# Which engine computes the first norm's adaLN columns: six columns from GpSimd to TensorE, and where the bias is added

## The chip, the cores and the metric

The kernel runs on one NeuronCore of a Trainium2 chip. The metric is device time in microseconds (us). Before the change it is 1839.2 us, the median of 3 runs (1838.87 to 1846.52). Engines are named as in the profile: PE is TensorE's matmuls and PEld its weight loads, DVE is VectorE, ACT ScalarE, POOL GpSimd, SP SyncE, which here only issues DMAs.

## The reference, cut to what matters

Two layers of a transformer over 128 context tokens and 512 latent tokens, 1024 features. Each layer first turns the two conditioning vectors (one for each stream) into shift, scale and gate, and each of its two norms is modulated by them:

```
mod = silu(cond) @ w_ada[l] + b_ada[l]           # 6 * 1024 values for each of two conds
sa, ca, ga, sf, cf, gf = split(mod, 6)
h = rmsnorm(x) * g_mix[l] * (1 + ca) + sa
p = h @ w_in[l]                                  # then attention, Fourier mixing, w_out, FFN
```

`sa` and `ca` of layer 0 (2 x 1024 values for each conditioning vector) are wanted before the first projection can begin.

## The kernel before, in words

Features lie on the 128 partitions, so a vector of 1024 values is eight columns, and the 6144 values of `mod` are 48 columns `mods[:, l, j]`, each with two entries (one a stream). Columns 0 to 7 are `sa`, 8 to 15 `ca`. A column needs a 128x1024 weight tile (512 KB) and can be computed in three ways.

- `ada_dve` (L146): two multiply-and-sum instructions on VectorE (L149; the trace calls them CUSTOM_DVE_ANT_0), then a 128x2 add of the bias on VectorE (L152).
- `ada_pool` (L156): two 128x1024 multiplications on GpSimd (L159), a sum over each product on ScalarE (L160), the bias on VectorE (L161).
- `ada_pe` (L165): eight fp32 matmuls with the weight tile as stationary operand and two moving columns (L168), into one PSUM tile; the bias on VectorE (L169). The trace shows such a matmul as two records, so a column is x16 there and x8 in the program's order.

At the start, `first()` loads x, sums its squares and computes the reciprocal roots (`stats`, L221). Then `norm_first` (L432) goes over the eight feature tiles k. For each, `before(k)` (L778) computes columns k and 8+k by the two letters of `ADA_ENG[k]` and folds the scale with the norm's gain (`make_gain`, L171). `modulate` (L242) writes the tile as two parts hi and lo (`hh_n`, `hl_n`), and 12 matmuls (`mm3`, L131 to L133) add this tile's part of the first two projections into the PSUM tiles `pk` and `pq`: two halves of the tokens, two projections, three products each. That is 96 matmuls of 320 or 322 columns, and `pk` and `pq` are complete only after the last. I call this the norm stage.

The weight tiles of the 16 columns take slots that attention uses later, seven at a time, in the order of `slots` (L775). SP issues the loads in its program order, and a load waits for its slot's last reader. The PSUM tiles of `ada_pe` alternate between two slots of one buffer each (tags `av` and `mm`).

The Tile framework's scheduler puts the instructions of the whole program in an order for each engine, and each engine then runs its list strictly in order. A change in one place can so reorder the lists elsewhere.

Two later places use the same helpers. In attention of layer 0, `gate` computes columns 16 to 23 with `ada_pe`. In `ffn(0)` the columns 24 to 39 are computed while the output projection (`wo`) runs, by `ADA2_ENG` alternately on VectorE and GpSimd; I call it the wo stage. It has two halves of tokens, with a `stats` between them (`ms` L229, `rs` L232, `rb` L234) whose result `rb` TensorE's matmul L237 waits for. The other columns, up to the whole of layer 1, are computed by `ada_dve` under the FFN.

Of the kernel before, what the change touches and what calls it, by code (L numbers as in the profile page):

```python
# [25 lines left out]
NL_TOK = 512  # L26
# token columns of a feature-major tile: ctx 0:128, two spare columns, latent 130:642
TW = 642
LO = 130
# the same with two zero columns at either end, for the convolution  # L30
HW = 646
# [6 lines left out]
FGROUPS = ((0, 8), (8, 8), (16, 6))  # L38
# head-key columns: latent 0:512, cache 512:640, ctx 640:768
KW = 768  # L40
# [5 lines left out]
def backbone_kernel(ctx: ExitStack, tc: tile.TileContext, A, O):  # L46
# [9 lines left out]

# [1 line left out]
    def const(name, shape):  # L58
# [20 lines left out]
    def late_consts(tmp):  # L79
        lam = tmp("lamv")[:, :L * 128].rearrange("p (l a d) -> p l a d", l=L, a=4)  # L80
        nc.sync.dma_start(out=lam, in_=A["lam"])
        for nm, sh in (("cos", [P, NL_TOK]), ("sin", [P, NL_TOK]), ("perm", [P, P]),
                       ("sel", [P, 2]), ("scv", [P, 1]), ("g_sub", [P, L]), ("g_kv", [P, L]),
                       ("g_ffn", [P, L, NK]), ("g_fin", [P, NK])):
            C[nm] = const(nm, sh)
        # lambda and the gain of the sub-norm, per layer
        lamt = tmp("lamt")[:, :L * 64].rearrange("p (l a d) -> p l a d", l=L, a=2)
        nc.vector.tensor_tensor(out=lamt, in0=lam[:, :, 0::2, :], in1=lam[:, :, 1::2, :], op=ALU.mult)
        lams = gp.tile([P, L, 2], F32, name="lams")
        nc.vector.tensor_reduce(out=lams, in_=lamt, axis=AX.X, op=ALU.add)  # L90
        nc.scalar.activation(out=lams, in_=lams, func=AF.Exp)
        neglam = gp.tile([P, L], F32, name="neglam")
        nc.vector.tensor_tensor(out=neglam, in0=lams[:, :, 1], in1=lams[:, :, 0], op=ALU.subtract)
        gs = gp.tile([P, L], F32, name="gs")
        for l in range(L):
            li = 0.8 - 0.6 * math.exp(-0.3 * l)
            nc.vector.tensor_scalar(out=neglam[:, l:l + 1], in0=neglam[:, l:l + 1], scalar1=-li, scalar2=None,
                                    op0=ALU.add)
            nc.vector.tensor_scalar(out=gs[:, l:l + 1], in0=C["g_sub"][:, l:l + 1], scalar1=1.0 - li, scalar2=None,
                                    op0=ALU.mult)  # L100
        C["neglam"], C["gs"] = neglam, gs

# [1 line left out]
    @contextmanager  # L104
# [9 lines left out]

    # the slots of weight tiles: two of each kind throughout, more in a phase that has the room
    def raw_tile(pool=None, bufs=2):
# [22 lines left out]

    # adaLN columns as per-partition scalars, on VectorE (features over partitions)  # L140
    def ada_cond(t):
# [4 lines left out]
    def ada_dve(l, j, wt, scond, junk):  # L146
        nc.sync.dma_start(out=wt, in_=A["w_adaT"][l, j])
        for c in range(2):
            nc.vector.tensor_tensor_reduce(  # L149
                out=junk, in0=wt, in1=scond[:, c], op0=ALU.mult, op1=ALU.add,  # L150
                scale=1.0, scalar=0.0, accum_out=mods[:, l, j, c:c + 1])
        nc.vector.tensor_scalar(out=mods[:, l, j], in0=mods[:, l, j], scalar1=bada[:, l, j:j + 1], scalar2=None,  # L152
                                op0=ALU.add)

    # the same on GpSimd and ScalarE
    def ada_pool(l, j, wt, scond, prod):  # L156
# [6 lines left out]

    # the same on TensorE, for some of the first layer's columns
    def ada_pe(j, wt, t):  # L165
        nc.sync.dma_start(out=wt, in_=A["w_ada0"][j])
        for k in range(NK):
            nc.tensor.matmul(t, lhsT=wt[:, 128 * k:128 * k + 128], rhs=scT[:, k], start=k == 0, stop=k == NK - 1)  # L168
        nc.vector.tensor_scalar(out=mods[:, 0, j], in0=t, scalar1=bada[:, 0, j:j + 1], scalar2=None, op0=ALU.add)  # L169

# [8 lines left out]

    # reciprocal root mean square of the columns of sq (features over partitions), one per  # L180
    # token, spread over the partitions: returns psum access patterns (ctx, latent)
    def rstd_bcast(sq, rhs, n, width, pool, eps=None, lat=None):
        """rhs [P, n]: which features a column sums."""
        pc, pl = tpt("rsc"), (lat or tpt)("rsl")
# [21 lines left out]

    # squares of the columns o:o+w of feature tile m: the first seven are summed in acc, the
    # last stays by itself
    def sumsq(acc, xm, m, pool, o, w, eng=None):
# [8 lines left out]

    # the statistics of half the columns (those before or from column bd): the reciprocal root
    # mean squares over the partitions, as (column, width, stream, psum access pattern)  # L220
    def stats(hf, bd, sqs, pool):  # L221
# [20 lines left out]

    # norm and modulation of half of feature tile k, into the tiles hi and lo
    def modulate(l, n, k, x, rb, hh, hl, pool, lo_pool=False):
# [18 lines left out]

# [1 line left out]
    def attention(l, xs, rb, close_x):  # L265
        with tc.tile_pool(name=f"at{l}", bufs=1, side="left", reuse_waits="tile") as ap, \
# [4 lines left out]
            mq = dp.tile([6, P, 2, TW], F32, name=f"mq_{l}")  # L271
            # rows 64 to 96 of a key hold the turned latent ones, rows 96 to 128 the others: nought elsewhere
            mk = dp.tile([6, P, 2, KW], F32, name=f"mk_{l}")
# [36 lines left out]

            # one 128-feature tile of the input projection, features over partitions
            def proj(j, wide=False, mid=None, dst=None, scale=None):
# [26 lines left out]

            # x32 columns: rotated latent 0:512, [cache], ctx, spare, raw latent  # L340
            def rotate(x32, lat0, j, pe=False):
# [88 lines left out]

            # the norm, with the first two projections on its heels
            def norm_first(before):  # L432
# [39 lines left out]

            # softmax numerators of one block of scores; their sums go to s_out
            def soft(s_in, p_out, s_out):
# [4 lines left out]

            # MLA: the normalised map. Differential: sum1 * (map1 - lambda * map2); sum1 stays in  # L480
            # the sums of the head and is allowed for in the epsilon of its norm.
            def combine(Ps, ss, w, qt):
# [18 lines left out]

            # scores(i, qt, tile) fills a psum tile with map i of query tile qt (4: ctx)
            def attend(nmap, scores, vv, p, e, of, sums=None):
# [115 lines left out]

            # keys and values of a pair of heads, in four steps  # L620
            def mla_kv(p):
# [55 lines left out]

            # Fourier mixing. The latent columns are folded by the symmetry of the transform over
            # positions: sums and differences of columns t and 512 - t, and of rows of the result.
            def fourier_u(mid):  # L680
# [14 lines left out]
            def fourier(u, oh, ol):  # L695
# [32 lines left out]
                for g in range(2):  # L728
# [10 lines left out]
                    w = slice(128 * g, 128 * g + 128)  # L739
                    # position 256 has no odd part: it goes where that of position 0, nought, lies  # L740
                    e = slice(1280, 1282)
# [20 lines left out]
            if l == 0:  # L762
# [10 lines left out]
                junk = ap.tile([P, 2 * 642], BF16, name="junk0", tag="t640", bufs=T640_BUFS)[:, :D]  # L773
                prod = ap.tile([P, 2, BW], F32, name="prod", tag="base", bufs=2)[:, :, :D]
                slots = iter((("VV", 6 * 256, NPAIR), ("ks", 2 * KW, 2), ("x32", BW, 2), ("VV", 6 * 256, NPAIR),  # L775
                              ("ks", 2 * KW, 2), ("x32", BW, 2), ("VV", 6 * 256, NPAIR)) * 3)

                def before(k):  # L778
                    for j, eng in zip((k, 8 + k), ADA_ENG[k]):
                        tag, n, b = next(slots)  # L780
                        t = ap.tile([P, n], F32, name="ada0", tag=tag, bufs=b)[:, :D]
                        if eng == "P":
                            ada_pe(j, t, (avt if j % 2 else mmt)("adaps")[:, :2])
                        elif eng == "V":
                            ada_dve(0, j, t, scond, junk)
                        else:
                            ada_pool(0, j, t, scond, prod)
                    make_gain(0, 0, k, k + 1)
# [65 lines left out]

# [1 line left out]
    xspill = dp.tile([NK, P, TW], F32, name="xspill")  # L856
# [12 lines left out]
    def first():  # L869
        xs, accs, close = x_pool("xin")  # L870
        # scratch: the slots of the tiles that the norm fills last
        class Pl:
# [182 lines left out]
PE_ROT = 1  # L1055
ADA_ENG = ('VG', 'GP', 'GV', 'GP', 'VV', 'PP', 'GV', 'PG')
T640_BUFS = 6
# [6 lines left out]

# [1 line left out]
def _split12(x):  # L1066
# [6 lines left out]
def _tables():  # L1073
# [3 lines left out]
    ang = {0: (t // 64).astype(f)[None, :] * inv[:, None], 1: (t % 64).astype(f)[None, :] * inv[:, None]}  # L1077
    # rows: half of a rotated pair, axis, frequency, then four blocks of 32 features
    blk = np.repeat(np.concatenate([ang[0], ang[1]] * 2, 0), 4, 0)
# [35 lines left out]

# the order of the rotated features: row (h, x, d, block) holds feature (block, x, h, d)
_ROT = np.arange(P).reshape(4, 2, 2, 8).transpose(2, 1, 3, 0).reshape(P)
# [78 lines left out]
```

## Time and profile before

| what | value |
|---|---|
| median of 3 runs | 1839.2 us |
| profiled execution, first to last instruction | 1843.6 us |
| PE busy | 1717.2 us (93%) |
| DVE busy | 1166.4 us (63%) |
| ACT busy | 779.4 us (42%) |
| POOL busy | 650.0 us (35%) |
| norm stage (end of the statistics' matmuls to the last of `pq`) | 19.6 to 74.2 us |
| wo stage on a saturated DVE | 394 to 460 us |

The page's span is the only time that the profiled execution has; it lies 4.4 us above the median of the runs. Starts in the rows are us from the span's start. A timeline row gives start, busy time, engine, line, operation, output and inputs, shapes and, in brackets, the idle time before it and what ended it. Busy times of pipelined matmuls overlap, so the pace of TensorE is read from one start to the next.

### The profile page before, as it was taken

What the parts mean: (1) busy time and instruction counts of PE and PEld (TensorE: products, weight loads), DVE (VectorE), ACT (ScalarE), POOL (GpSimd) and SP (SyncE); (2) the same over time, 40 slices, a digit from 0 to 9 for tenths busy, and PEclk for the clock granted to TensorE, in tenths of its full rate; (3) what the DMA queues carried; (4) which work ended last, traced back from release to release, by engine and by line L of the source; (5) the groups of instructions that cost most, each with busy time, mean ns of one, the idle gap of its engine ahead of it and who ended that gap; (6) DMA issues with size and microseconds to landing.
All of it is one profiled execution on the core that took longest, in us unless ns stands there. A gap on an engine that the chain in (4) does not pass through costs nothing. (4 is left out here: it accounts for less than half of the span.)

```text
span 1843.6 us, 29032 instructions
## 1 busy us (share of the span) xinstructions
PE 1717.2 (93%) x11160; PEld 1670.1 (91%) x11160; DVE 1166.4 (63%) x2051; ACT 779.4 (42%) x1494; POOL 650.0 (35%) x719
## 2 busy tenths in 40 slices
PE   6988899986999999999999798999999999999997
PEld 5878899876899999999998787998999999999997
DVE  7628765679799999734455388865544434443445
ACT  5436564643543123313343466765433313321332
POOL 6547454548422112201242576562212201220222
PEclk9889898988899999999999899999999999999998
DMA  7367654655255565322254576562312222222223
GB/s 279 96 210 208 193 172 149 207 175 171 82 182 172 183 202 164 111 73 73 63 169 135 177 214 183 176 205 73 103 35 74 76 72 78 70 81 69 78 69 118
DMA packets 81084, 249.70 MB, mean 135 GB/s; under 512 B 10417, under 2 KB 19761, under 8 KB 79281
## 3 DMA queue, kind: packets, MB, share of 16 engines
q1 hardware_dynamic: 74226, 209.13, 35.6%
q0 software_dynamic: 6720, 38.72, 7.6%
q8 instruction: 88, 1.44, 0.3%
q14 instruction: 50, 0.41, 0.1%
HBM read 203.43 MB, written 41.24 MB: 133 GB/s over the span
## 5 line engine op out<-in xcount | busy, mean ns | idle before, releaser
L132 PE MATMUL up<-hl_o,whi 128*128 128x324 f32 x1408 | 441.2, 314 | 2.7 <-POOL hl_o L113 2.7
L131 PE MATMUL up<-hh_o,whi 128*128 128x324 f32 x1408 | 440.4, 314 | 2.3 <-ACT hh_o L260 1.2
L133 PE MATMUL up<-hh_o,wlo 128*128 128x324 f32 x1408 | 440.8, 314 | 0.0
L112 ACT CAST whi<-raw 128x1024 fp32r<-128x1024 f32 (+2 forms) x210 | 207.0, 989 | 434.7 <-PE dn L132 204.7
L113 DVE TENSOR_TENSOR wlo<-raw,whi 128x1024 fp32r<-128x1024 f32 (+2 forms) x184 | 227.0, 1237 | 203.4 <-ACT whi L112 199.2
L990 POOL TENSOR_TENSOR cg<-cg,cv 128x644 f32<-128x644 f32 x44 | 73.2, 1664 | 665.4 <-DVE cv L986 653.9
L132 PEld LDWEIGHTS up<-hl_o,whi 128*128 128x128 f32 x1408 | 268.0, 190 | 4.4 <-POOL hl_o L113 4.3
L131 PEld LDWEIGHTS up<-hh_o,whi 128*128 128x128 f32 x1408 | 267.8, 191 | 3.0 <-ACT hh_o L112 1.6
L133 PEld LDWEIGHTS up<-hh_o,wlo 128*128 128x128 f32 x1408 | 267.1, 190 | 0.0
L131 PE MATMUL dn<-gh,whi 128*128 128x322 f32 x704 | 218.7, 314 | 5.0 <-ACT gh L112 3.9
L132 PE MATMUL dn<-gl,whi 128*128 128x322 f32 x704 | 220.1, 313 | 0.0
L133 PE MATMUL dn<-gh,wlo 128*128 128x322 f32 x704 | 218.9, 313 | 0.0
L149 DVE CUSTOM_DVE_ANT_0 junk<-ada,scond 128x1024 bf16<-128x1024 f32 x138 | 199.4, 1445 | 4.4 <-ACT scond L143 2.8
L477 DVE TENSOR_REDUCE nm<-sc 128x1 f32<-128x640 f32 (+1 forms) x180 | 126.5, 711 | 76.5 <-PE sc L576 56.2
L478 ACT ACTIVATE P<-sc,nm 128x640 f32<-128x640 f32 (+1 forms) x180 | 128.1, 713 | 74.9 <-DVE nm L477 56.6
L859 DVE SCALAR_TENSOR_TENSOR x_x<-dn,mods,x_x 128x128 f32<-128x128 f32 (+2 forms) x144 | 57.6, 436 | 132.8 <-PE dn L133 132.7
L131 PEld LDWEIGHTS dn<-gh,whi 128*128 128x128 f32 x704 | 133.4, 190 | 6.9 <-ACT gh L112 4.1
L133 PEld LDWEIGHTS dn<-gh,wlo 128*128 128x128 f32 x704 | 133.8, 190 | 0.4 <-DVE wlo L113 0.4
L132 PEld LDWEIGHTS dn<-gl,whi 128*128 128x128 f32 x704 | 133.9, 190 | 0.3 <-POOL gl L113 0.2
L131 PE MATMUL proj<-hh_n,whi 128*128 128x320 f32 (+1 forms) x320 | 109.0, 341 | 5.7 <-ACT whi L112 3.0
L133 PE MATMUL proj<-hh_n,wlo 128*128 128x320 f32 (+1 forms) x320 | 106.8, 334 | 0.0
L132 PE MATMUL proj<-hl_n,whi 128*128 128x320 f32 (+1 forms) x320 | 106.5, 333 | 0.0
(299 smaller groups left out, 3740.0 us busy)
## 6 DMA issues: line engine op xcount, KB each, us to landing
raw<-in_w_up SPq DMA_DIRECT2D x88, 512.0 KB, 3.6
ada<-in_w_adaT SPq DMA_DIRECT2D x83, 512.0 KB, 3.6
raw<-in_w_down SPq DMA_DIRECT2D x32, 512.0 KB, 3.6
raw<-in_w_in SPq DMA_DIRECT2D x28, 512.0 KB, 4.9
raw<-in_w_down SPq DMA_DIRECT2D x32, 384.0 KB, 3.2
qs<-dq POOLq DMA_DIRECT2D x12, 865.5 KB, 9.1
ks<-mk POOLq DMA_DIRECT2D x12, 768.0 KB, 4.9
raw<-in_w_out SPq DMA_DIRECT2D x16, 512.0 KB, 4.5
```

The source lines that it names most:

```text
L112: nc.scalar.copy(out=hi, in_=src)
L113: (lo_eng or nc.vector).tensor_tensor(out=lo, in0=src, in1=hi.bitcast(F32), op=ALU.subtract)
L131: nc.tensor.matmul(out, lhsT=lh, rhs=rh, start=first, stop=False)
L132: nc.tensor.matmul(out, lhsT=lh, rhs=rl, start=False, stop=False)
L133: nc.tensor.matmul(out, lhsT=ll, rhs=rh, start=False, stop=last)
L149: nc.vector.tensor_tensor_reduce(out=junk, in0=wt, in1=scond[:, c], op0=ALU.mult, op1=ALU.add, scale=1.0, scalar=0.0, accum_out=mods[:, l, ...
L477: nc.vector.tensor_reduce(out=nm, in_=s_in, axis=ax, op=ALU.max, negate=True)
L478: nc.scalar.activation(out=p_out, in_=s_in, func=AF.Exp, bias=nm, scale=1.0, accum_out=s_out)
L859: nc.vector.scalar_tensor_tensor(out=x[:, o:o + w], in0=ps, scalar=gate, in1=x[:, o:o + w], op0=ALU.mult, op1=ALU.add)
L990: nc.gpsimd.tensor_tensor(out=c[0], in0=c[0], in1=c[1], op=ALU.mult)
```

## The change

`ADA_ENG` gives eleven of the sixteen columns to TensorE, five to VectorE (as before) and none to GpSimd; before it was five, five and six. `ada_dve` passes the bias as the initial value of its sums in place of 0.0, so L152 goes everywhere (5 in the norm stage, 8 in the wo stage, 56 more). `ada_pe` adds the bias on ScalarE, as an Identity activation that reads PSUM (new L167), also for the eight columns of `gate`. `ada_pool` stays in the wo stage as it was. Comments go, so line numbers move by two to five.

```diff
@@ ada_dve
             nc.vector.tensor_tensor_reduce(
                 out=junk, in0=wt, in1=scond[:, c], op0=ALU.mult, op1=ALU.add,
-                scale=1.0, scalar=0.0, accum_out=mods[:, l, j, c:c + 1])
-        nc.vector.tensor_scalar(out=mods[:, l, j], in0=mods[:, l, j], scalar1=bada[:, l, j:j + 1], scalar2=None,
-                                op0=ALU.add)
+                scale=1.0, scalar=bada[:, l, j:j + 1], accum_out=mods[:, l, j, c:c + 1])
@@ ada_pe
-        nc.vector.tensor_scalar(out=mods[:, 0, j], in0=t, scalar1=bada[:, 0, j:j + 1], scalar2=None, op0=ALU.add)
+        nc.scalar.activation(out=mods[:, 0, j], in_=t, func=AF.Identity, bias=bada[:, 0, j:j + 1], scale=1.0)
@@ attention, before(k)
-                prod = ap.tile([P, 2, BW], F32, name="prod", tag="base", bufs=2)[:, :, :D]
...
                         if eng == "P":
                             ada_pe(j, t, (avt if j % 2 else mmt)("adaps")[:, :2])
-                        elif eng == "V":
+                        else:
                             ada_dve(0, j, t, scond, junk)
-                        else:
-                            ada_pool(0, j, t, scond, prod)
@@
-ADA_ENG = ('VG', 'GP', 'GV', 'GP', 'VV', 'PP', 'GV', 'PG')
+ADA_ENG = ('VP', 'PP', 'PV', 'PP', 'VP', 'PV', 'PP', 'PV')
```

The first place is PE at the start of the norm stage, from the last statistics to the first projection matmuls (`rsh` and `rb` are the statistics, `adaps` the columns' PSUM tile, `ada` their weight tile). Before:

```order
L226 MATMUL rsh<-ones,sq_123 128x1
L168 MATMUL adaps<-c_condT,ada_264 128x2 x8
L237 MATMUL rsh<-ident,rb_136 128x128 x2
L237 MATMUL rsh<-ident,rb_136 128x63
L237 MATMUL rsh<-ident,rb_152 128x128 x2
L237 MATMUL rsh<-ident,rb_152 128x65
L131 MATMUL pk<-hh_n_171,whi 128x320
L131 MATMUL pq<-hh_n_171,whi 128x320
```

The same place now, up to the same two matmuls:

```order
L224 MATMUL rsh<-ones,sq_123 128x1
L166 MATMUL adaps<-c_condT,ada_205 128x2 x7
L235 MATMUL rsh<-ident,rb_136 128x128 x2
L235 MATMUL rsh<-ident,rb_136 128x63
L166 MATMUL adaps<-c_condT,ada_205 128x2
L166 MATMUL adaps<-c_condT,ada_260 128x2 x3
L235 MATMUL rsh<-ident,rb_152 128x128 x2
L235 MATMUL rsh<-ident,rb_152 128x65
L166 MATMUL adaps<-c_condT,ada_260 128x2 x5
L166 MATMUL adaps<-c_condT,ada_318 128x2 x8
L131 MATMUL pk<-hh_n_171,whi 128x320
L131 MATMUL pq<-hh_n_171,whi 128x320
```

Where one column stood ahead of the first projection matmul, three stand now. The second place is PE between the first and the second feature tile (`hh_n_171` and `hh_n_172`), as one piece of the difference:

```order
 L132 MATMUL pq<-hl_n_179,whi 128x322
 L133 MATMUL pq<-hh_n_171,wlo 128x322
+L166 MATMUL adaps<-c_condT,ada_272 128x2 x6
+L166 MATMUL adaps<-c_condT,ada_425 128x2 x8
+L166 MATMUL adaps<-c_condT,ada_366 128x2 x8
+L166 MATMUL adaps<-c_condT,ada_517 128x2 x8
 L131 MATMUL pk<-hh_n_172,whi 128x320
 L131 MATMUL pq<-hh_n_172,whi 128x320
-L168 MATMUL adaps<-c_condT,ada_447 128x2 x4
```

Nearly four columns come here in one stretch, with no projection matmul among them. The third place is DVE between the two halves of the wo stage, from the statistics `ms` to `rb` (`x2_x0`, `x3_x0` are residual tiles). Before:

```order
L229 TENSOR_SCALAR ms_4686<-rsh_4679 128x3
L152 TENSOR_SCALAR mods_81<-mods_81,c_b_ada_66 128x2
L149 ISA junk_4302,mods_81<-ada_4667,scond_4299 128x1024
L149 ISA mods_81 128x1
L859 SCALAR_TENSOR_TENSOR x2_x0_4279<-wo_4857,mods_81,x2_x0_4279 128x320
```

The same place now, with the new kernel's line numbers:

```order
L227 TENSOR_SCALAR ms_4702<-rsh_4695 128x3
L149 ISA junk_4326,mods_81<-ada_4684,scond_4323,c_b_ada_66 128x1024
L149 ISA mods_81 128x1
L854 SCALAR_TENSOR_TENSOR x2_x0_4303<-wo_4873,mods_81,x2_x0_4303 128x320
L149 ISA junk_4326,mods_81<-ada_4684,scond_4323,c_b_ada_66 128x1024
```

The 128x2 bias add is gone from DVE's list and the multiply-and-sum reads `c_b_ada` itself.

## Rows read from the trace of the kernel before

**Rows 1.** Busy time by stretch: length, PE, PEld, DVE, ACT, POOL, granted clock, DMA

```profile
19.60:35.60 16.00, 6.24 (x28) 6.05 (x28) 15.85 (x23) 4.40 (x10) 14.51 (x16) 1.00 0.90 334
35.60:74.20 38.60, 35.57 (x160) 34.26 (x160) 35.30 (x80) 21.17 (x48) 20.63 (x13) 0.82 0.18 60
394.00:460.00 66.00, 43.22 (x262) 41.77 (x261) 65.77 (x72) 26.50 (x46) 58.67 (x40) 0.83 0.53 177
```

**Rows 2.** Timeline of PE in the norm stage

```profile
19.00 0.57 PE L226 MATMUL rsh<-ones,sq 128*128 128x1 f32 x2
20.28 3.57 PE L168 MATMUL adaps<-c_condT,ada 128*128 128x2 f32 x16 [0.71 <-DMA ada<-in_w_ada]
23.71 2.80 PE L237 MATMUL rsh<-ident,rb 128*128 128x128 f32 x12
35.62 0.64 PE L131 MATMUL pk<-hh_n,whi 128*128 128x320 f32 x1 [9.10 <-ACT hh_n L260]
...
40.80 0.47 PE L131 MATMUL pk<-hh_n,whi 128*128 128x322 f32 x1
41.07 0.47 PE L131 MATMUL pq<-hh_n,whi 128*128 128x322 f32 x1
...
51.71 0.36 PE L132 MATMUL pq<-hl_n,whi 128*128 128x322 f32 x1
51.91 0.31 PE L133 MATMUL pq<-hh_n,wlo 128*128 128x322 f32 x1
54.35 1.96 PE L168 MATMUL adaps<-c_condT,ada 128*128 128x2 f32 x12 [2.13 <-DVE mods L169]
...
60.16 0.64 PE L132 MATMUL pk<-hl_n,whi 128*128 128x322 f32 x1 [0.65 <-DVE hl_n L261]
...
62.37 3.58 PE L168 MATMUL adaps<-c_condT,ada 128*128 128x2 f32 x16 [0.24 <-DVE mods L169]
65.80 0.61 PE L132 MATMUL pk<-hl_n,whi 128*128 128x320 f32 x1
...
69.04 0.31 PE L132 MATMUL pk<-hl_n,whi 128*128 128x320 f32 x1
69.19 0.31 PE L133 MATMUL pk<-hh_n,wlo 128*128 128x320 f32 x1
...
73.92 0.30 PE L133 MATMUL pq<-hh_n,wlo 128*128 128x322 f32 x1
```

**Rows 3.** Costliest groups of DVE, 14 to 74 us

```profile
L149 DVE CUSTOM_DVE_ANT_0 junk<-ada,scond 128x1024 bf16<-128x1024 f32 x10 | 20.8, 2081 | 0.1
```

**Rows 4.** Line L149 in the whole run: ns min/median/max

```profile
L149 DVE CUSTOM_DVE_ANT_0 junk<-ada,scond x138: 1204/1214/3414, 14.1 to 752.4; 128x1024 bf16<-128x1024 f32 x138
```

**Rows 5.** Line L166, the loads of TensorE's columns: landing

```profile
DMA to landing us min/median/max: 3.4/4.4/9.7
```

**Rows 6.** Timeline of ACT: a small activation, and the end of the norm stage

```profile
36.88 0.20 ACT L91 ACTIVATE lams<-lams 128x4 f32<-128x4 f32 x1
...
73.82 0.83 ACT L112 CAST whi<-raw 128x768 fp32r<-128x768 f32 x1 [3.37 <-PE pk L132]
```

**Rows 7.** Costliest groups of DVE, 394 to 460 us

```profile
L149 DVE CUSTOM_DVE_ANT_0 junk<-ada,scond 128x1024 bf16<-128x1024 f32 x16 | 32.4, 2024 | 2.6 <-ACT scond L143 2.5
L152 DVE TENSOR_SCALAR mods<-mods,c_b_ada 128x2 f32<-128x2 f32 x8 | 10.1, 1262 | 0.0
```

**Rows 8.** Waits, 394 to 476 us: us in total, times, longest

```profile
PE rsh L237 <- DVE rb L234: 10.7, 1, 10.7
```

**Rows 9.** Timeline of DVE in the wo stage

```profile
432.79 2.44 DVE L152 TENSOR_SCALAR mods<-mods,c_b_ada 128x2 f32<-128x2 f32 x1
434.94 1.22 DVE L149 CUSTOM_DVE_ANT_0 junk<-ada,scond 128x1024 bf16<-128x1024 f32 x1
```

**Rows 10.** Line L152 in the whole run: ns min/median/max

```profile
L152 DVE TENSOR_SCALAR mods<-mods,c_b_ada x69: 207/220/2440, 18.8 to 754.5; 128x2 f32<-128x2 f32 x69
```

**Rows 11.** Timeline of POOL beside rows 9

```profile
431.84 3.17 POOL L159 TENSOR_TENSOR prod<-ada,scond 128x1024 f32<-128x1024 f32 x1
```

## The prediction

> **What bounds the kernel now.** The page comes first: PE is busy nearly all the time, but its share is an average over stages. The chain of waits does not reach back into the first layer, so I read the stages that the change touches with the busy time by stretch, then the timelines of the engines that wait there.
>
> In the norm stage, 19.6 to 74.2 us, PE is busy 6.24 + 35.57 = 41.8 of 54.6 us [rows 1]. The idle 12.8 us are five gaps in PE's timeline: 0.71, 9.10, 2.13, 0.65 and 0.24 us [rows 2]. Behind four of them stands DVE: it makes the tiles that `hh_n` is cast from, the `hl_n`, and the bias adds that free the PSUM tile of a column. DVE is busy 15.85 of the first 16.0 us [rows 1]. That is no honest work: ten multiply-and-sums took 20.8 us [rows 3], and one undisturbed takes 1.21 us [rows 4], so 20.8 - 12.1 = 8.7 us went into blocking by POOL's multiplications, which fill 14.51 of the same 16 us [rows 1]. So the stage is bound by DVE at its start, and by PE and DVE in turn after 35.6 us, where PE has 3.7 of the 12.8 us idle.
>
> What a column costs on PE is the distance from its first matmul to the next instruction: 20.28 to 23.71 and 62.37 to 65.80, both 3.43 us [rows 2]. The level of the clock is read from the pace of the projection matmuls: 0.27 us from start to start at 40.80, 320 columns, which is 1.2 GHz, and 0.15 us at 69.04, near 2.4 GHz [rows 2]. (The column of the granted clock reads 1.00 for 19.6 to 35.6 us and 0.82 after [rows 1]; for the first stretch I go by the durations.) PE ran without a gap from 35.62 to 51.71 us, two columns among its matmuls, and the clock was low throughout; it rose after a run of projection matmuls alone, was low again in the column at 62.37, and rose for good about 3.1 us into the last run, which began at 65.80 [rows 2].
>
> In the wo stage, 394 to 460 us, DVE is busy 65.77 of 66 us and PE 43.22 [rows 1]. PE's longest wait is one of 10.7 us for `rb` [rows 8].
>
> **The change part by part.** *The norm stage.* GpSimd's twelve multiplications and ScalarE's twelve sums go. DVE keeps its five columns and loses 16 bias adds and the 8.7 us of blocking, so its tiles come early. In the new order three columns stand ahead of the first projection matmul, at 19.6 + 3 x 3.43 + 2.8 (the `ident` matmuls [rows 2]) = 32.7 us; by then the first tile should be there: column 8 is done near 24.4 us, and what DVE still owes it (two multiply-and-sums of 1.21 us and a few short instructions) takes some 4 us. So I take all 12.8 us of PE's idle time as gone. In its place come six columns on PE, 6 x 3.43 = 20.6 us, and nothing runs beside them on that engine. PE then works from 19.6 to 19.6 + 41.8 + 20.6 = 82.0 us, 7.8 us later than now.
>
> The clock shifts this a little. Now the upper level saves some 36 matmuls x 0.12 us = 4.3 us in the last run, and about 0.9 us around 51.7 and 54.35 us (the twelve records there take 1.96 us where sixteen take 3.5 [rows 2]). In the new order 58 projection matmuls follow the last column. If the clock again rises 3.1 us into them, 12 run at 0.27 and 46 at 0.15 us: 5.5 us saved. One run of 16 projection matmuls earlier may lift it once more, for up to 1.7 us. I take 0.8 us better than now: the stage ends at 81.2 us, term +7.0. Its ends: +13 if the clock never rises (7.8 + 5.2), and -12 if it is up all the time (rival 2).
>
> Three things could put idle time back into PE; I cost them at nothing. The bias on ScalarE is 0.20 us by the nearest row [rows 6], eleven times 2.2 us on an engine busy 4.40 + 21.17 of 54.6 us [rows 1] that sheds twelve sums. The PSUM tiles alternate, so a bias add has the 3.43 us of the next column; only columns 5 and 7 follow each other in one tile, with two matmuls between: up to 0.5 us. The load of column 7 waits for the slot of column 11, done near 59 us by my sum, and is wanted near 67: landing takes 4.4 us in the median and 9.7 at most [rows 5], so 0 to 2 us. The seed read by the multiply-and-sum I take at 0; were it the 0.2 us of the add that it replaces, DVE's room would cover it.
>
> The term carries over one to one: ACT's next weight cast waits for `pk` until 73.82 us [rows 6], and the loads and projections behind it hang on `pk` and `pq` in the same way. I see no wait on anything else that could swallow it.
>
> *The wo stage.* Eight bias adds leave DVE's list. They took 10.1 us [rows 7], but one undisturbed takes 0.22 us [rows 10]. The rest is in [rows 9, 11]: the add at 432.79 stood 2.44 us, until POOL's multiplication (431.84 + 3.17 = 435.0 us) ended, and the multiply-and-sum behind it then ran in its clean 1.22 us. Without the add that multiply-and-sum would have stood there itself. So the two ends are 8 x 0.22 = 1.8 us and 10.1 us of DVE's time; of PE's time nothing to 10.7 us, the wait for `rb` [rows 8]. I take -3.0 us, near the lower end, since the same POOL work stays and the new order moves one multiply-and-sum into the path from the last residual to `ms` (+1.2 us or more), while two adds leave the path from `ms` to `rb`.
>
> The Trainium skill (SBUF — State Buffer, section Who interferes with whom) says that VectorE and GpSimd take a shared pair of ports as an exclusive lock for a whole instruction, so that the other one stands until its end. By that rule a wait passes on to the next instruction that needs the pair and the term would be -1.8 us; by the durations of the rows alone it would be -10.1 us. The trace agrees with the rule here [rows 9, 11].
>
> *The rest.* Under the FFN 56 more adds go from a DVE that PE does not wait for: 0. In `gate` eight adds move to ScalarE: 8 x 0.20 = 1.6 us at most, beside PE's work; I take +0.3. The scheduler has also reordered the lists of attention in both layers. No row prices that; a single wait that moved cost up to 10.7 us [rows 8], and many small swaps should cancel: 0, with -5 and +5 as ends.
>
> *The sum.* +7.0 - 3.0 + 0.3 = +4.3 us on the profiled 1843.6 us, which is 4.4 us over the median of the runs. Against the median the same share gives 1839.2 x (1 + 4.3 / 1843.6) = 1843.5 us.
>
> **The rivals.**
>
> 1. *The wo stage gives its whole 10.1 us.* For it: DVE is full there and PE waits 10.7 us. Against it: the blocked time is POOL's, which stays. Then 7.0 - 10.1 = -3 us: 1836 us.
>
> 2. *TensorE's clock stays up, and the columns cost half.* With no idle time PE's stream is dense from 19.6 us. At 2.4 GHz its work, (41.8 + 5.2 + 20.6) / 2 = 34 us, would end at 54; then DVE bounds with 51.2 - 8.7 = 42.5 us [rows 1, 3, 4], to 62 us: -12, and with the wo stage -15: 1824 us. For it: the clock did rise twice. Against it: 16 gapless microseconds with two columns in them did not raise it [rows 2], and now whole stretches are columns alone.
> The Trainium skill (TensorE: Matmul & The Clock Gate, section Why this matters for your kernels) advises keeping TensorE continuously busy to get its full clock, and by that rule this rival would be the likely one. The trace does not bear it out for columns: they ran at the low level at 20.28 and 62.37.
>
> 3. *Slower: the last run stays slow.* The 58 projection matmuls come after a stretch of columns. If the clock rises only near their end, the 5.5 us are lost, the stage term is +13, and with a wo stage that gives 1 us or nothing the time is 1852 us. It decides from where the clock rises 4 us later than in my sum, past 78 us. For it: low level at 60.16 and 65.80 after mixed work. Against it: the last run is longer than the one that raised the clock now.
>
> **How the numbers follow.** My forecast 0.62, with its own range 1838 to 1849; rival 1 0.13; rival 2 0.07; rival 3 0.18. A change under 0.5% (9.2 us) can't be told from none here. Faster than 1830.0: rival 2 and a tail of rival 1, 0.10. Slower than 1848.4: most of rival 3 and a tail of mine, 0.18. The rest is 0.72. The range 1832 to 1851 leaves out rival 2 and the upper part of rival 3.
>
> **What would show it.** PE with under 1.5 us idle from 19.6 us to the last `pq`; that matmul near 81 us; whole columns at 3.4 us; the multiply-and-sums of the norm stage all near 1.2 us; the first `hh_n` cast done before PE asks for it. In the wo stage, PE's wait for `rb` at 6 to 9 us. I am wrong if columns take 1.7 us, if the last `pq` comes before 76 or after 84 us, or if the shift seen at the end of the stage is gone by the start of the wo stage.

## The result, and the profile after

The changed kernel takes 1859.1 us (median of 4 runs, 1854.2 to 1861.9), the kernel before 1839.7 us beside it: a ratio of 1.0098, 95% interval [1.0073, 1.0122]. That is slower by about 1%, 19 us between the medians; the forecast was 4.3 us slower. The two profiled spans, 1860.1 and 1843.6 us, lie 16.5 us apart. Where they part is read from the starts of TensorE's first matmul of each stage:

| stretch of TensorE's timeline | before, us | after, us | difference |
|---|---|---|---|
| start to the last `pq` of layer 0 | 73.9 | 77.6 | +3.7 |
| from there to the first `proj` | 48.4 | 47.2 | -1.2 |
| attention of layer 0 (first `proj` to first `wo`) | 261.2 | 276.2 | **+15.0** |
| wo stage and second norm (first `wo` to first `up`) | 89.1 | 87.5 | -1.6 |
| FFN of layer 0 (first `up` to the first `pq` of layer 1) | 501.5 | 499.7 | -1.8 |
| first norm of layer 1 (to its first `vps`) | 18.1 | 18.1 | 0.0 |
| attention of layer 1 (first `vps` to first `wo`) | 294.0 | 297.0 | **+3.0** |
| the rest | 557.4 | 556.8 | -0.6 |

The norm stage first, in busy time by stretch of the kernel after (columns as in [rows 1]):

```profile
19.60:35.60 16.00, 16.00 (x74) 16.00 (x74) 9.69 (x28) 3.62 (x8) 2.21 (x10) 1.00 0.91 321
35.60:74.20 38.60, 38.60 (x188) 38.59 (x187) 21.22 (x57) 12.24 (x36) 5.58 (x7) 0.82 0.20 65
```

TensorE, the first pair of numbers after the length, has no idle time left where it had 12.8 us [rows 1], and VectorE (the third pair) has fallen from 51.2 to 30.9 us. Its multiply-and-sums, the costliest groups of VectorE from 14 to 78 us, are no longer blocked: 13.3 us for ten where [rows 3] has 20.8.

```profile
L149 DVE CUSTOM_DVE_ANT_0 junk<-ada,scond,c_b_ada 128x1024 bf16<-128x1024 f32 x10 | 13.3, 1331 | 5.4 <-DMA ada<-in_w_adaT 5.3
```

TensorE's timeline of the stage shows the columns (L166, sixteen records each) and the pace of the projections:

```profile
36.29 12.80 PE L166 MATMUL adaps<-c_condT,ada 128*128 128x2 f32 x60
48.95 0.61 PE L131 MATMUL pk<-hh_n,whi 128*128 128x320 f32 x1
...
54.76 0.47 PE L131 MATMUL pk<-hh_n,whi 128*128 128x322 f32 x1
55.03 0.39 PE L132 MATMUL pk<-hl_n,whi 128*128 128x322 f32 x1
...
55.86 6.89 PE L166 MATMUL adaps<-c_condT,ada 128*128 128x2 f32 x44
62.61 0.61 PE L131 MATMUL pk<-hh_n,whi 128*128 128x320 f32 x1
...
72.05 0.41 PE L132 MATMUL pq<-hl_n,whi 128*128 128x322 f32 x1
72.30 0.31 PE L133 MATMUL pq<-hh_n,wlo 128*128 128x322 f32 x1
...
77.64 0.31 PE L133 MATMUL pq<-hh_n,wlo 128*128 128x322 f32 x1
```

The 60 records from 36.29 take 3.4 us a column, as before [rows 2]. At 55.03, after 19 projection matmuls with four records of a column among them, the pace goes from 0.27 to 0.15 us: the clock rises, and the 44 column records behind it take 6.75 us where the low level makes 44 / 16 x 3.38 = 9.3. It is low again by 62.61 and rises for good at 72.05, 5.5 us into the last run, which began at 66.56.

Now attention of layer 0, by stretch, in the kernel before and in the kernel after:

```profile
122.30:383.50 261.20, 241.57 (x1643) 229.38 (x1643) 177.38 (x350) 157.12 (x361) 135.93 (x165) 0.92 0.58 179
```

```profile
124.80:401.00 276.20, 248.46 (x1644) 234.62 (x1643) 179.80 (x342) 157.45 (x369) 136.37 (x165) 0.91 0.54 165
```

The counts of TensorE agree within one record: the work is the same. Its idle time is 276.20 - 248.46 = 27.7 us and was 19.6, and its busy time, which for equal work is a matter of its pace, is 6.9 us longer. Further profiles below show how far both vary for one and the same list. TensorE's waits in this stretch (us in total, times, longest), before and then after, show no single place:

```profile
PE sc L573 <- ACT P L478: 4.3, 6, 1.8
PE proj L131 <- ACT whi L112: 3.0, 1, 3.0
...
PE sc L570 <- ACT P L478: 1.7, 2, 1.0
```

```profile
PE sc L571 <- ACT P L476: 6.6, 8, 2.0
PE av L541 <- DVE tl L113: 3.8, 5, 1.8
PE sc L131 <- ACT P L476: 3.5, 3, 2.8
PE sc L568 <- ACT P L476: 2.9, 2, 2.6
```

The matmuls of scores (`sc`) wait 13.0 us for a softmax (`P`) in the kernel after; in the kernel before it was 6.0 on the same two lines and 0.3 more on L131.

### The profile page after: what moved, and what is told of

Its sections match the earlier page's. It is cut to its first block, busy times and chain, and to the rows that moved or that the text cites. A ratio compares the mean times of both kernels' runs of the same rounds, so it can differ in the third digit from the quotient of the medians.

```text
span 1860.1 us, 29175 instructions
## 1 busy us (share of the span) xinstructions
PE 1739.0 (93%) x11256; PEld 1693.3 (91%) x11256; DVE 1141.6 (61%) x1963; ACT 769.4 (41%) x1489; POOL 613.0 (33%) x707
## 5 line engine op out<-in xcount | busy, mean ns | idle before, releaser
L131 PE MATMUL up<-hh_o,whi 128*128 128x324 f32 x1408 | 441.0, 314 | 2.3 <-ACT hh_o L258 1.2
L131 PEld LDWEIGHTS up<-hh_o,whi 128*128 128x128 f32 x1408 | 267.7, 190 | 3.2 <-ACT hh_o L112 1.7
L149 DVE CUSTOM_DVE_ANT_0 junk<-ada,scond,c_b_ada 128x1024 bf16<-128x1024 f32 x138 | 216.7, 1570 | 12.5 <-DMA ada<-in_w_adaT 9.1
L131 PE MATMUL dn<-gh,whi 128*128 128x322 f32 x704 | 218.9, 314 | 4.7 <-ACT gh L112 3.6
L131 PEld LDWEIGHTS dn<-gh,whi 128*128 128x128 f32 x704 | 133.4, 190 | 6.6 <-ACT gh L112 3.8
L131 PE MATMUL proj<-hh_n,whi 128*128 128x320 f32 (+1 forms) x320 | 108.1, 338 | 3.0 <-DVE VVm L649 1.3
L113 DVE TENSOR_TENSOR tl<-tp,th 128x512 fp32r<-128x512 f32 x144 | 88.2, 618 | 28.9 <-ACT th L112 27.4
```

Source lines behind the costliest of these rows:

```text
L113: (lo_eng or nc.vector).tensor_tensor(out=lo, in0=src, in1=hi.bitcast(F32), op=ALU.subtract)
L131: nc.tensor.matmul(out, lhsT=lh, rhs=rh, start=first, stop=False)
L149: nc.vector.tensor_tensor_reduce(out=junk, in0=wt, in1=scond[:, c], op0=ALU.mult, op1=ALU.add, scale=1.0, scalar=bada[:, l, j:j + 1], accu ...
```

## The experiments

All ratios are to the kernel before, timed beside each on the same chip. The loss was to be split between three theories. A: the order of the instructions in attention, which the scheduler made anew. B: the bias of the gate columns on ScalarE. C: the longer norm stage and what it delays. To try A, the order was held: at the end of the program, edges that set only the order of issue were added between neighbours of a recorded list (`ORDER`), from the end of the norm stage on. The instructions are those of the kernel that is named, and so are their waits for data.

```diff
+    traced, last, at = list(nc.cur_bb.bb.instructions), None, 0
+    for d in np.frombuffer(zlib.decompress(base64.b85decode(ORDER)), np.uint16):
...
+        if last is not None:
+            tc.add_manual_dep(traced[at], last.name, mybir.DependencyInfo(
+                mybir.DependencyClass.NoSync, mybir.DependencyReason.DATA), reason="order")
+        last = traced[at]
```

**The new work in the old order, and the old work in the new.** The edit is the block above, in the changed kernel with the recorded lists of the kernel before, and the other way round.

> The changed kernel, but every engine's instructions from the end of the norm stage on stand in the order that the kernel before has (the norm stage keeps its new order). Theory A, the order of the attention lists is what costs the 15 us between the first wide projection (109.0 us) and the first matmul of the wo stage (401.0): attention takes 277 us again as before, within 4; what is left is the norm stage (+3.7) and the wo stage (-1.6), so a ratio of 1.001 (1.000 to 1.003). Theory B, the bias of the gate columns on ScalarE costs it (it holds the PSUM slot of the projections): that work is still there, so attention stays at 288 to 292 us and the ratio is near 1.009. Theory C, the longer norm stage (later loads, a clock that starts elsewhere) costs it: the same, near 1.009.

> The kernel before, but from the end of the norm stage on in the order that the changed kernel has; columns, biases and engines are all as before. Theory A (order): attention takes 288 to 292 us, the ratio is 1.006 to 1.009. Theory B (gate bias on ScalarE) and theory C (norm stage): 1.000, attention 277 us.

Measured: 0.9979 [0.9965, 0.9994] (1836.0 us) and 1.0141 [1.0116, 1.0166] (1865.3 us). Attention of layer 0 by stretch, of the first and then of the second:

```profile
123.20:379.40 256.20, 235.83 (x1644) 223.20 (x1643) 173.88 (x342) 158.18 (x369) 135.34 (x165) 0.94 0.57 178
```

```profile
122.10:395.50 273.40, 245.76 (x1644) 231.75 (x1643) 178.27 (x350) 156.01 (x361) 136.78 (x165) 0.92 0.55 171
```

The length goes with the order and not with the work, in both directions: 256 us in the old order, 273 in the new. Theory A stands; B and C are out as causes of the 15 us. Both ratios went further than I had given (1.000 to 1.003, and 1.006 to 1.009). B has a small true part: in the first run TensorE's waits hold one for the gate's bias on ScalarE,

```profile
PE proj L133 <- ACT mods L169: 2.4, 1, 2.4
```

**Each half of the change, in an order of its own.**

The first has the new `ADA_ENG`, and in `ada_dve` and `ada_pe`, against the changed kernel,

```diff
-                scale=1.0, scalar=bada[:, l, j:j + 1], accum_out=mods[:, l, j, c:c + 1])
+                scale=1.0, scalar=0.0, accum_out=mods[:, l, j, c:c + 1])
+        nc.vector.tensor_scalar(out=mods[:, l, j], in0=mods[:, l, j], scalar1=bada[:, l, j:j + 1], scalar2=None,
+                                op0=ALU.add)
...
-        nc.scalar.activation(out=mods[:, 0, j], in_=t, func=AF.Identity, bias=bada[:, 0, j:j + 1], scale=1.0)
+        nc.vector.tensor_scalar(out=mods[:, 0, j], in0=t, scalar1=bada[:, 0, j:j + 1], scalar2=None, op0=ALU.add)
```

The second has these lines as the change writes them, and the old `ADA_ENG` with its six columns on GpSimd.

> The new table of engines alone (eleven columns on TensorE, none on GpSimd); all biases are added on VectorE as before, no seed. The scheduler makes an order of its own, unlike either. Theory B: no gate bias on ScalarE, so attention is back to 277 us and the ratio is 1.002 (norm stage +3.7). Theory C: the norm stage is the new one, so 1.008 or more. Theory A: the norm stage ends 3 to 4 us later as in the changed kernel, and attention takes anything from 272 to 292 us by its own order: 0.998 to 1.010, and no more than that can be said ahead.

> The two bias edits alone (seeded sums, bias on ScalarE in the norm stage and in the gate); the table of engines is as before, with six columns on GpSimd. Its order in attention is close to that of the kernel before on TensorE. Theory B: the gate bias on ScalarE costs 12 to 15 us, 1.007. Theory C: the norm stage is the old one, so 0.998 to 1.000. Theory A: an order near the old one, so attention within 5 us of 277, with the wo stage -1.6: 0.997 to 1.002.

Measured: 1.0144 [1.0124, 1.0164] and 1.0146 [1.0130, 1.0163]. Each half alone is slower than both together. The second has the old norm stage, which speaks against C once more. Both missed theory A's expectation (0.998 to 1.010, and 0.997 to 1.002), the second by far: I had taken a list that is close to the old one on TensorE in layer 0 as safe. Layer 0 took 267.6 us, and layer 1, where I had not looked, 308.1 where it was 294.0. How close a list is does not tell its price: in layer 1 some 1600 of TensorE's 1734 matmul records stand in their old order in this run, and some 1430 in the changed kernel, which took 297.0 us there.

**Each half in the old order.** The same two kernels, with the block.

> The new table of engines alone, biases on VectorE as before; from the end of the norm stage on every engine's list stands in the old order. With the order held, this run and the next one split what the changed work is worth (both together gave 0.9979). Theory A1, the terms of the forecast: eleven columns on TensorE make the norm stage end 2 to 4 us later, and the gain is all in the biases: 1.001 to 1.002. Theory A2, the later end is made good behind it (the weight loads of attention have more time, GpSimd is free earlier): 0.998 or less. Theory C of the first runs (the longer norm stage costs 15 us): 1.008.

> The two bias edits alone (seeds; bias on ScalarE in the norm stage and in the gate), the old table of engines, old order from the end of the norm stage on. Theory A1: the wo stage gains 2 to 3 us and the norm stage a little: 0.996 to 0.998. Theory A2: nothing, 0.999 to 1.001. Theory B (gate bias on ScalarE costs in attention): a wait of TensorE for that bias of 2.4 us as in the first run, 1.001. Against the same work in its own order (1.0146) it tells once more what the order costs: 1.5% if theory A holds.

Measured: 1.0017 [1.0005, 1.0029] and 0.9969 [0.9955, 0.9984], theory A1. With the order held, the engines cost 3.1 us (0.9 to 5.3) and the biases give 5.7 us (2.9 to 8.3). Part of the gain is in the wo stage, from the first `wo` to the first `up`: 86.0 us with the biases, 89.5 with the engines alone, 89.1 before. TensorE's waits there show it, in the biases' run and then in the engines' run [rows 8]:

```profile
PE rsh L237 <- DVE rb L234: 8.1, 1, 8.1
```

```profile
PE rsh L239 <- DVE rb L236: 10.7, 1, 10.7
```

**Which list: TensorE's in one layer, then in both.** The block again in the changed kernel, with no other edit than the data: `ORDER` holds TensorE's instructions of attention alone, of layer 0 in the first run and of both layers in the second.

> The changed kernel with one list held in the old order: TensorE's, in the attention of layer 0. The other four engines, and all of layer 1, are ordered by the scheduler as it likes. Theory A, narrowed to this list: attention of layer 0 takes 256 to 262 us from the first projection to the wo stage (276.2 in the changed kernel, 261.2 before), the ratio is 1.000 to 1.004. If the loads, VectorE's or ScalarE's order, or layer 1 carry the loss: 1.007 or more.

> The changed kernel with TensorE's list in the attention of both layers held in the old order; the other four engines, the wo stage and the FFN are ordered by the scheduler. If TensorE's list carries the whole loss: attention of layer 0 in 256 to 262 us and of layer 1 in 292 to 296, and 0.997 to 1.000 of the kernel before, as with all lists held (0.9979). If the lists of the other engines carry a part of it, 1.002 or more.

Measured: 1.0060 [1.0039, 1.0081] and 0.9974 [0.9956, 0.9991]. With one layer held, the stretches of layer 0 and of layer 1 are

```profile
119.60:377.20 257.60, 238.53 (x1645) 225.82 (x1643) 173.12 (x342) 158.14 (x369) 135.64 (x165) 0.93 0.57 177
...
981.90:1289.90 308.00, 273.58 (x1735) 255.74 (x1735) 194.61 (x360) 169.88 (x395) 161.89 (x185) 0.91 0.56 170
```

Layer 0 is back at 257.6 us with nothing but TensorE's list held. This does not show that the other engines' lists have no part: with TensorE's held, the scheduler wrote those of ScalarE, GpSimd and SyncE in layer 0 just as in the old order, by the tiles that the traces name, and VectorE's with five instructions out of 342 in other places. Whether TensorE's list does it alone or with the lists that follow from it was not tried. The ratio is above the range that I gave, since the scheduler now wrote another list for layer 1, and that costs 14 us against the old one. With both held the loss is gone. Layer 1 took 299.1 us in that profile, 5 more than in the old order of all engines (292 to 296 was expected). There too the other lists differ from the old ones in a few places only, and the ratio shows no loss, so these 5 us stay unexplained.

**A better split of the columns.** With the order held, the norm stage can be tried by itself: eight columns each on TensorE and VectorE, and seven and nine (the second line added).

```diff
-ADA_ENG = ('VP', 'PP', 'PV', 'PP', 'VP', 'PV', 'PP', 'PV')
+ADA_ENG = ('VP', 'VP', 'PV', 'PV', 'VP', 'VP', 'PV', 'PV')
+ADA_ENG = ('VP', 'VP', 'PV', 'PV', 'VP', 'VV', 'PV', 'PV')
```

> The changed kernel with eight columns on TensorE and eight on VectorE, a column of each kind for every feature tile, old order from the end of the norm stage on. Three columns of 3.43 us leave TensorE; VectorE, busy 31 of 54.6 us in the changed kernel, takes three of 2.43 us. Theory D, TensorE alone bounds the norm stage: it ends 5 to 10 us earlier than in the changed kernel (68 to 73 us), and the whole is 0.993 to 0.997 of the kernel before. Theory E, VectorE's tiles come late and TensorE idles instead: the stage ends at 75 to 78, 0.998.

> Seven columns on TensorE and nine on VectorE, old order held. With eight and eight VectorE was busy 36 of the 40 us from 19.6 to 60 us and TensorE idle for one gap of 1.1 us. Theory E': VectorE bounds the norm stage now, so the ninth column (2.4 us there) takes back what TensorE saves: the last matmul of the stage at 62 to 66 us, 0.990 to 0.993. Theory D': TensorE still bounds it, 59 to 61 us, 0.989.

Measured: **0.9910 [0.9889, 0.9932]** (1823.7 us against 1840.2) and 0.9931 [0.9905, 0.9958]. The first is a version that beats both kernels. The last `pq` of its norm stage starts at 63.2 us; by stretch and on TensorE's timeline the stage reads

```profile
19.60:35.60 16.00, 16.00 (x74) 16.00 (x75) 15.65 (x42) 7.29 (x18) 5.65 (x14) 1.00 0.90 325
35.60:63.50 27.90, 26.77 (x165) 26.33 (x163) 21.75 (x55) 8.71 (x24) 2.36 (x3) 0.86 0.25 89
```

```profile
38.17 0.46 PE L133 MATMUL pk<-hh_n,whi 128*128 128x322 f32 x1
38.44 0.34 PE L134 MATMUL pk<-hl_n,whi 128*128 128x322 f32 x1
...
41.01 5.03 PE L168 MATMUL adaps<-c_condT,ada 128*128 128x2 f32 x42
...
52.56 0.39 PE L133 MATMUL pk<-hh_n,whi 128*128 128x320 f32 x1
52.79 0.31 PE L133 MATMUL pq<-hh_n,whi 128*128 128x320 f32 x1
...
60.97 0.41 PE L133 MATMUL pk<-hh_n,whi 128*128 128x320 f32 x1 [1.13 <-ACT hh_n L260]
```

VectorE is now busy 37.4 of 43.9 us and TensorE idle once, for 1.1 us: the two are nearly even. That is theory D, and it ends 5 us earlier than I gave: the clock rises at 38.44 already, the 42 column records behind it take 1.9 us a column, and the projections are at the upper pace again from 52.56 to 62.3. With seven columns the last `pq` came at 61.7, between what D' and E' gave (59 to 61, 62 to 66), so neither is shown. The two stages cannot be ranked by these profiles either: with eight and eight, TensorE runs the same stage in the same order in two later runs, and there the last `pq` came at 65.6 and 66.1. The time was not shorter: attention of layer 0 took 263.5 us in the profile with seven columns, the slowest of its six runs, against 258.9. The intervals overlap; which of the two is better stays open.

**Eight and eight in an order of its own, and with the gate's bias on VectorE.** The first is without the block; the second has it, and in `ada_pe`

```diff
+        if j < 16:
             nc.scalar.activation(out=mods[:, 0, j], in_=t, func=AF.Identity, bias=bada[:, 0, j:j + 1], scale=1.0)
+        else:
+            nc.vector.tensor_scalar(out=mods[:, 0, j], in0=t, scalar1=bada[:, 0, j:j + 1], scalar2=None, op0=ALU.add)
```

> The eight-and-eight version (0.991 with the old order held) with the order that the scheduler makes for it. Its norm stage is the same and gains 10 us. Theory A: a new draw of the attention lists costs 3 to 30 us as in the four kernels with an order of their own so far (1.0098, 1.0144, 1.0146, and 1.006 with one list held), so 0.993 to 1.007, and not 0.991. If the lists were a matter of this change alone, 0.991.

> The eight-and-eight version with the old order held, but the bias of the eight gate columns back on VectorE, as before the change. Theory B in its small form: the wait of TensorE for that bias on ScalarE goes (2.4 us in the first run), 0.989 to 0.990 of the kernel before. Rival: the wait is only passed on (another instruction holds the slot), 0.991 as without this edit.

Measured: 0.9993 [0.9978, 1.0008] and 0.9907 [0.9875, 0.9938]. The scheduler's own list takes back all that the split gains. The gate's bias on VectorE makes no difference that can be told (0.9907 against 0.9910): what is left of theory B is below what these runs can tell.

**All orders together.** The same work with the old lists and with others:

| work | old lists | lists of the scheduler or of the changed kernel |
|---|---|---|
| kernel before | 1 | 1.0141 |
| changed kernel | 0.9979 | 1.0098 |
| engines alone | 1.0017 | 1.0144 |
| biases alone | 0.9969 | 1.0146 |
| eight and eight | 0.9910 | 0.9993 |

The profiles agree. With all the old lists (seven profiles, the kernel before among them) attention takes 254.3 to 263.5 us in layer 0 and 293.7 to 297.0 in layer 1; with other lists 267.6 to 276.2 (five profiles) and 296.5 to 308.1 (six). In layer 0 the two groups stand apart. In layer 1 they touch: the changed kernel's list took 297.0 us there, and 296.5 with the old work, so the 3.0 us of the first table are not told from the spread. TensorE alone, in attention of layer 0: with its old list (nine profiles) it is idle 17.3 to 20.4 us and busy 235.8 to 244.7; with other lists idle 20.6 to 27.7 and busy 244.5 to 249.1. So both the waits and the pace carry the loss.

**What such a list does** is seen at one place of layer 0, in TensorE's timeline of the changed kernel and then of the same work in the old order (`av` multiplies the softmax with the values, `proj` is the input projection, which waits for no softmax; rows left out where marked):

```profile
308.81 0.31 PE L133 MATMUL proj<-hh_n,wlo 128*128 128x322 f32 x1
309.65 2.20 PE L166 MATMUL ada2p<-c_condT,raw 128*128 128x2 f32 x16 [0.53 <-ACT qn L336]
...
317.91 0.28 PE L541 MATMUL av<-tl,VVm 128*128 128x256 f32 x1
321.02 0.41 PE L131 MATMUL sc<-ks,qs 128*128 128x320 f32 x1 [2.83 <-ACT P L476]
...
321.67 0.47 PE L131 MATMUL sc<-ks,qs 128*128 128x320 f32 x1
321.93 0.47 PE L132 MATMUL sc<-ks,qs 128*128 128x320 f32 x1
...
326.55 0.31 PE L131 MATMUL proj<-hh_n,whi 128*128 128x320 f32 x1
```

```profile
304.76 0.28 PE L543 MATMUL av<-tl,VVm 128*128 128x256 f32 x1
304.87 0.31 PE L133 MATMUL proj<-hh_n,whi 128*128 128x320 f32 x1
...
307.56 0.31 PE L133 MATMUL proj<-hh_n,whi 128*128 128x320 f32 x1
307.71 0.31 PE L133 MATMUL sc<-ks,qs 128*128 128x320 f32 x1
```

After the same run of eight `av` the new list has scores that must wait 2.83 us for a softmax, and what follows runs at 0.27 us, the low level of the clock. The old list has 19 projection matmuls there, and the scores behind them wait for nothing and keep the pace of 0.15. In the new list one group of projections had ended at 308.81, and the next stands only behind these scores, at 326.55. This is one place of many; how much of the 15 us each holds was not separated.

## Why the prediction was wrong, step by step

- *What bounds the stage; idle time and columns.* Right: no idle time from 19.6 us to the last `pq` (under 1.5 us was asked), columns at 3.4 us, multiply-and-sums at 1.3 us. (A slip without consequence: of the 12.8 us of idle time before, 3.0 lay after 35.6 us and not 3.7, by [rows 1].)
- *The clock in the stage (0.8 us better, term +7.0).* The mechanism was right, the size off: the stage ended 3.7 us later. The earlier run raised the clock for longer than the "up to 1.7 us" allowed for, since the columns behind it ran at the upper level too for a while (2.5 us saved, and 0.6 on five projections). In the last run the clock rose after 5.5 us and not 3.1, which left 38 matmuls at the upper pace in place of 46 (4.5 us). That is 7.6 us saved where it was 5.2 before: 2.4 better, not 0.8. The other 1.7 us were not traced. The size is also a matter of the run: three of the experiments have the changed kernel's list on TensorE up to the last `pq`, and there the last `pq` came at 76.3, 76.3 and 72.2 us, the last of these outside the 76 to 84 that I gave. With the order held the engines cost 3.1 us in all.
- *It carries over one to one.* In part: +3.7 at the last `pq`, +2.5 at the first `proj`, then buried. With the same work in the old order it was +2.4 and +0.9, and behind that the spread of attention (254 to 264 us with the old lists) hides it. One to one is not shown.
- *The wo stage, -3.0.* Right: -1.6 in the changed kernel, -3.1 with the biases alone and the old order; the wait for `rb` fell from 10.7 [rows 8] to 8.1 us (6 to 9 was said). Rival 1, the whole 10.1 us, did not come. The adds left VectorE's list, but the multiply-and-sums there took longer than in [rows 7] (32.4 us):

```profile
L149 DVE CUSTOM_DVE_ANT_0 junk<-ada,scond,c_b_ada 128x1024 bf16<-128x1024 f32 x16 | 35.5, 2218 | 2.6 <-ACT scond L143 2.5
```

  Of these 3.1 us, 1.0 is the start value that they now read (sixteen times 0.065 us, see the last section). The other 2.1 us I read as a part of the wait, passed on to them. The Trainium skill (SBUF — State Buffer, section Who interferes with whom) says that the ports which VectorE and GpSimd share are an exclusive lock, so that the one that comes second stands still; the trace agrees: beside GpSimd's work these sixteen took 2.2 us each, where the median of the whole run is 1.28.
- *Gate bias, +0.3.* Not refuted: one wait of 2.4 us in TensorE's waits, no difference in the time.
- **The rest: "many small swaps should cancel: 0, with -5 and +5 as ends".** This is the step that failed. The new lists cost 15.0 us in layer 0, up to 3.0 in layer 1, and 1.2% of the time (22 us) by the two ratios of the changed kernel. The swaps do not cancel: of four lists that the scheduler wrote anew for layer 0 none came up to the old one. For layer 1 it also wrote four (engines alone and eight and eight got the same one): two took 308 us and one 299.8 and 302.0, where all the old lists took 293.7 to 297.0 and TensorE's old list with others 299.1; the changed kernel's, with 297.0 and 296.5, is not told from the old. The runs do not tell how the old list came about. I had taken my ends from a single wait that moved, where two lists of some 1700 matmuls each were written anew.
- *The rivals.* None held. Rival 3 names the right sign for a reason that did not occur (the last run did reach the upper level); rival 2's columns at half price occurred for a part of one stretch.
- *The sum.* With the old lists held the change is 0.21% faster (0.06 to 0.35), where the forecast was 0.23% slower: the engines cost less than half of the +7.0 and the biases gave some 3 us more than the -2.7.

## What to carry to other kernels

Where a scheduler orders the whole program, an edit has two effects: its own work, and a new draw of every list behind it. The second was 0.8 to 1.8% here, more than any term of the edit, so price it as a loss with a wide range where the old lists are good; every one of the five pairs here was a loss. Hold the old order to measure the edit itself (here 0.998 instead of 1.010), and keep it held to bank what is found (0.991 instead of 0.999).

## What the runs showed of the hardware that I had not expected

- In 12.7 us of columns alone (60 records from 36.29 us in the changed kernel) the clock did not rise. Where a run of projections had raised it, the columns behind went on at the upper level for a while: 42 records from 41.01 us with eight and eight took 1.9 us a column, which mixes both levels, against 3.4 at the low one.
- The same list of TensorE does not get the clock at the same moment in every run. In the run with one layer held, the norm stage has the changed kernel's list on TensorE and no idle time either, but the clock rose at 36.25 us, within the run of 12 projection matmuls behind which the changed kernel was still at the low level, and those 60 records took 9.7 us:

```profile
36.25 0.34 PE L135 MATMUL pq<-hh_n,wlo 128*128 128x322 f32 x1
36.42 9.81 PE L168 MATMUL adaps<-c_condT,ada 128*128 128x2 f32 x60
46.09 0.61 PE L133 MATMUL pk<-hh_n,whi 128*128 128x320 f32 x1
...
72.23 0.30 PE L135 MATMUL pq<-hh_n,wlo 128*128 128x322 f32 x1
```

  The stage ended 5.4 us earlier than in the changed kernel, more than the 3.7 us between the kernels before and after. One profile does not measure a stage whose length hangs on the clock.
- A multiply-and-sum whose start value is read from a tile takes longer: its line's durations (min/median/max) are now

```profile
L149 DVE CUSTOM_DVE_ANT_0 junk<-ada,scond,c_b_ada x138: 1265/1279/3411, 14.0 to 766.1; 128x1024 bf16<-128x1024 f32 x138
```

  against 1214 ns in the median [rows 4]: two times 0.065 us a column, beside the 0.22 us of the add that it replaces.
